# Depthwise convolution of block 2 taken off GpSimd, two channel tiles moved ahead of the attention loop, gates spread anew

## Chip, cores and metric

The kernel runs on 1 core of a Trainium2 chip. The metric is the device time of one launch in microseconds (us). The engines are called by the names of the profile: PE (TensorE), DVE (VectorE), ACT (ScalarE), POOL (GpSimd) and SP (SyncE, whose queue starts most transfers).

## What is computed

Two transformer blocks run one after the other on 512 tokens of width 1024. The change lies in the first half of the second one (`second_block`, one layer). Cut to what matters:

```python
h = modulate(rms_norm_2(x, norm1_g), sh1, sc1)
u = h @ w_in                       # queries, keys/values, conv branch, gates
qn, qr = mla_queries(u[..., :256], q_norm_g, w_uq)          # rms_norm of 256 columns, then w_uq
kn, kr, v = mla_keys(u[..., 256:416], kv_norm_g, w_ukv)     # rms_norm of 128 columns, then w_ukv
attn = attend_blocked(qn, qr, kn, kr, v)                    # 16 heads, 512 queries, 768 keys

a, g = split(u[..., 416:2464])                              # conformer_conv, 1024 channels
y = a * sigmoid(g)
y = depthwise_conv(y, conv_w, 31 taps, centred) + conv_b
y_c = silu(layer_norm(y, ln_g, ln_b)) @ w_pw

g = sigmoid(u[..., 2464:])                                  # 2 x 1024 gates
x = x + g1 * ((g[:1024] * (attn @ w_o_mla) + g[1024:] * y_c) @ w_out)
```

After it comes a product-key expert layer, which the change does not touch.

## The kernel before

Activations lie transposed: 128 channels of a tile on the partitions, the 512 tokens along the free axis. Every float32 matrix product is made from three passes: operand and weight are split into a high part (a copy rounded to fp32r, made by ACT in `split`, L120) and a low part (the difference, made by DVE or POOL in `sub`, L115 or L113), and `lin` runs 8 x 3 = 24 matmuls of 512 columns for one 128-channel output tile. Below, such a group of 24 is called a projection. `load_w` brings a weight tile of 128x1024 through SP and splits it.

`block2` has a prologue, a loop and a tail.

- **Prologue.** The norm of the input is applied (`norm_out`); the key/value latent is projected, its inverse root is made (`rstd`, with ACT's square root and one Newton step on DVE, `newton` L184 to L189) and broadcast over the partitions by small matmuls (`row`, L216). Then come the rotary key, two query tiles `cq` (L886) with a second inverse root, and their splits.
- **Loop.** 16 heads with two units each (`unit`, 256 queries). A unit runs scores on PE, the row maximum on DVE (`mx`, L999), the exponential and the division by the sum on ACT (`pr`), transposes on PE, splits of the transposed weights (`pt`), the product with the values, and one addition into `rc` (L1027), the last DVE instruction of a unit. `prep` makes query, key and value operands of the next head between two units.
- **Filler of the loop.** Twice in a unit, `fill` runs one entry of the list `taps`, and once in a unit one entry of the list `jobs`. The jobs of a channel tile of the convolution are `conv_g` (projection, sigmoid into `y`), `conv_a` (projection, product into `y`) and one or two of the 16 gate projections (`gate`). `conv_a` puts 8 entries on `taps`, each with 2 of the first 16 taps on DVE (L924, L926, summed in place in `z`, the tile `Y` of the profile) and 2 of the other 15 on POOL (a product with a broadcast weight, L929, and an addition, L931). The last entry adds the two halves and adds the tile to `zsum`, on POOL (L933 to L937). Gates in the loop have their low weight part made by POOL (L113).
- **Tail.** Gates that are left run, 3 of them before the layer norm of the convolution and 3 after it; then three stages of eight projections: `w2_omla`, `w2_pw` and `w2_out`.

The order in which the instructions stand on each engine is set when the program is built: a scheduler reorders instructions of the program text within what dependencies and buffers allow. Each engine then runs its own list strictly in that order. The constants that the change touches say how many taps stay on DVE, how many channel tiles get a second gate, and how many gates stay behind the layer norm:

```python
NCV = 16
NGA = 2
NGB = 3
```

Of the kernel before, what the change touches and what calls it, by code (L numbers as in the profile page):

```python
# [8 lines left out]
F32 = mybir.dt.float32  # L9
# [9 lines left out]
P = 128  # L19
# [53 lines left out]
class Kern:  # L73
# [743 lines left out]
    def block2(self, res, r1, r2):  # L817
# [81 lines left out]

        taps = []  # L900

        def conv_g(ct):
            w = self.load_w(a["w2_conv"][8 + ct])
            pg = self.pt("F")
            self.lin([(pg, lat)], w, hh, hl)
            y = self.t(bi, [P, SEQ + 30], F32, "y", bufs=2)
            nc.gpsimd.memset(y[:, :15], 0.0)
            nc.gpsimd.memset(y[:, 15 + SEQ:], 0.0)
            nc.scalar.activation(y[:, 15:15 + SEQ], pg, AF.Sigmoid)
            ys[ct] = y  # L910

        def conv_a(ct):
            w = self.load_w(a["w2_conv"][ct])
            pa = self.pt("F")
            self.lin([(pa, lat)], w, hh, hl)
            y = ys[ct]
            nc.vector.tensor_tensor(y[:, 15:15 + SEQ], pa, y[:, 15:15 + SEQ], op=ALU.mult)  # L917
            zc = z[:, ct]
            zp = self.t(bi, [P, 2, SEQ], F32, "zp")

            def tap(i):
                for j in range(2 * i, min(2 * i + 2, NCV)):
                    if j == 0:
                        nc.vector.tensor_scalar(zc, y[:, :SEQ], cw[:, ct, 0:1], cb[:, ct:ct + 1], op0=ALU.mult, op1=ALU.add)  # L924
                    else:
                        nc.vector.scalar_tensor_tensor(zc, y[:, j:j + SEQ], cw[:, ct, j:j + 1], zc, op0=ALU.mult, op1=ALU.add)  # L926
# [11 lines left out]
            for i in range(8):  # L938
                taps.append(lambda i=i: tap(i))
# [725 lines left out]
```

## Time and profile before

| what | us |
|---|---|
| median of 3 runs (lowest, highest) | 2815.07 (2813.57, 2820.57) |
| the profiled execution: its own time | 2819.39 |
| the profiled execution: span of its trace | 2817.6 |
| PE busy in the span | 2590.9 (92%) |
| DVE busy in the span | 2097.3 (74%) |
| ACT busy in the span | 1196.2 (42%) |
| POOL busy in the span | 1018.9 (36%) |

The rows below come from that one execution. Stretches are given in us from the start of its span. A duration in a row of the timeline reaches a little into the next instruction's start, so the time that an instruction takes from its engine is read from one start to the next.

### The profile page before, as it was taken

The page shows a single profiled execution, that of the slowest core. Times are in us where ns is not written, and L with a number is a line of the kernel's source. Part 1 is how long each engine was busy: PE and PEld are TensorE (multiplying, and loading weights), DVE is VectorE, ACT ScalarE, POOL GpSimd, SP SyncE. Part 2 cuts the span into 40 slices and gives each one's busy share as a digit, 9 for nine tenths or more (in the row PEclk, how much of TensorE's full clock was granted, in tenths as well). Part 3 has the DMA queues.
Part 4 walks back from the last instruction along what each step waited for, and adds up shares of the span by engine and source line. Part 5 has one row for each costly group of instructions (what it writes and reads, how often), then busy time and mean ns, then how long its engine had stood idle before and what let it go on. Part 6 is the DMA issues. An engine that isn't in the chain of part 4 may idle for free. (4 is left out here: it accounts for less than half of the span.)

```text
span 2817.6 us, 38436 instructions
## 1 busy us (share of the span) xinstructions
PE 2590.9 (92%) x14307; PEld 2246.0 (80%) x14307; DVE 2097.3 (74%) x3521; ACT 1196.2 (42%) x1839; POOL 1018.9 (36%) x714
## 2 busy tenths in 40 slices
PE   7899999999988888889998998788899999999998
PEld 6788888887866677777877887777788888888887
DVE  7646677774358898996558777999687888877875
ACT  4445442333245566666342222566433333333332
POOL 0001101110008888882005455554243444444430
PEclk9999999999999999999999999999999999999999
DMA  3210257663331111114433333678999999999993
GB/s 123 70 52 16 91 166 216 215 211 123 114 97 55 51 47 46 50 42 139 144 119 119 116 122 110 227 272 268 326 347 339 340 342 337 339 324 339 332 320 135
DMA packets 218660, 509.99 MB, mean 181 GB/s; under 512 B 23916, under 2 KB 97048, under 8 KB 218344
## 3 DMA queue, kind: packets, MB, share of 16 engines
q1 hardware_dynamic: 168344, 352.23, 37.9%
q0 software_dynamic: 37568, 136.42, 13.8%
q10 hardware_dynamic: 12560, 18.88, 1.8%
q8 instruction: 112, 1.84, 0.3%
q14 instruction: 76, 0.62, 0.1%
HBM read 457.12 MB, written 50.33 MB: 180 GB/s over the span
## 5 line engine op out<-in xcount | busy, mean ns | idle before, releaser
L120 ACT ACTIVATE whi<-wraw 128x1024 fp32r<-128x1024 f32 (+2 forms) x315 | 324.2, 1029 | 597.0 <-PE psU L156 143.5
L115 DVE TENSOR_TENSOR wlo<-wraw,whi 128x1024 fp32r<-128x1024 f32 (+2 forms) x227 | 282.7, 1245 | 155.5 <-ACT whi L120 146.3
L158 PE MATMUL psU<-X,wlo 128*128 128x384 f32 (+1 forms) x1032 | 356.5, 346 | 17.2 <-DVE wlo L115 12.8
L154 PE MATMUL psU<-X,whi 128*128 128x384 f32 (+1 forms) x1032 | 355.5, 345 | 10.3 <-ACT whi L120 8.9
L156 PE MATMUL psU<-Z,whi 128*128 128x384 f32 (+1 forms) x1032 | 354.4, 343 | 0.0
L113 POOL TENSOR_TENSOR wlo<-wraw,whi 128x1024 fp32r<-128x1024 f32 x88 | 222.1, 2526 | 147.3 <-ACT whi L120 143.0
L1169 POOL DMA_INDIRECT row<-v_rows,rsf x128 | 177.0, 1383 | 244.5 <-DVE Y L1188 211.7
L1169 POOL DMA_INDIRECT row<-u_rows,rsf x128 | 167.7, 1310 | 266.7 <-DVE Y L1181 234.3
L120 ACT ACTIVATE wh<-s 128x384 fp32r<-128x384 f32 x128 | 66.9, 525 | 442.5 <-DVE s L1428 436.9
L1446 PE MATMUL psV<-vl,wh 128*128 128x512 f32 x768 | 236.6, 389 | 0.0
L1446 PE MATMUL psV<-vh,wh 128*128 128x512 f32 x768 | 236.5, 389 | 0.0
L1446 PE MATMUL psV<-vh,wl 128*128 128x512 f32 x768 | 236.4, 389 | 0.0
L158 PEld LDWEIGHTS psU<-X,wlo 128*128 128x128 f32 x1032 | 197.5, 191 | 22.1 <-DVE wlo L115 15.2
L154 PEld LDWEIGHTS psU<-X,whi 128*128 128x128 f32 x1032 | 196.7, 191 | 18.1 <-ACT whi L120 12.3
L156 PEld LDWEIGHTS psU<-Z,whi 128*128 128x128 f32 x1032 | 196.7, 191 | 2.8
L1188 DVE SCALAR_TENSOR_TENSOR Y<-row,ckr,Y 128x1024 f32<-128x1024 f32 x128 | 164.0, 1281 | 31.8 <-DMA row<-v_rows,rsf 30.5
L931 POOL TENSOR_TENSOR zp<-zp 128x512 f32<-128x512 f32 x112 | 176.0, 1572 | 8.6
L929 POOL TENSOR_TENSOR zp<-y,cw 128x512 f32<-128x512 f32 x120 | 155.4, 1298 | 63.5 <-DVE y L917 48.4
L1181 DVE SCALAR_TENSOR_TENSOR Y<-row,Y 128x1024 f32<-128x1024 f32 x128 | 158.1, 1235 | 22.8 <-DMA row<-u_rows,rsf 21.9
L1446 PEld LDWEIGHTS psV<-vl,wh 128*128 128x128 f32 x768 | 144.2, 188 | 29.9
L1446 PEld LDWEIGHTS psV<-vh,wl 128*128 128x128 f32 x768 | 144.2, 188 | 29.9
L115 DVE TENSOR_TENSOR vl<-vraw,vh 128x1024 fp32r<-128x1024 f32 x128 | 156.3, 1221 | 13.8 <-ACT vh L120 13.7
(562 smaller groups left out, 6535.7 us busy)
## 6 DMA issues: line engine op xcount, KB each, us to landing
wraw<-w_u SPq DMA_DIRECT2D x128, 512.0 KB, 4.5
vraw<-w_v SPq DMA_DIRECT2D x128, 512.0 KB, 6.6
wraw<-w_mod SPq DMA_DIRECT2D x64, 512.0 KB, 4.2
g_dram<-gs SPq DMA_DIRECT2D x96, 256.0 KB, 5.3
gg<-g_dram SPq DMA_DIRECT2D x32, 768.0 KB, 9.7
wraw<-w_up SPq DMA_DIRECT2D x44, 512.0 KB, 3.6
s_dram<-s ACTq DMA_DIRECT2D x64, 192.0 KB, 1.9
s<-s_dram SPq DMA_DIRECT2D x64, 192.0 KB, 8.1
```

What stands on the lines that cost most here:

```text
L113: self.nc.gpsimd.tensor_tensor(dst, x, f(hi), op=ALU.subtract)
L115: self.nc.vector.tensor_tensor(dst, x, f(hi), op=ALU.subtract)
L120: nc.scalar.activation(hi, src, AF.Copy)
L154: nc.tensor.matmul(o, wh, xh[:, c], start=first, stop=False)
L156: nc.tensor.matmul(o, wh, xl[:, c], start=False, stop=False)
L158: nc.tensor.matmul(o, wl, xh[:, c], start=False, stop=last)
L929: nc.gpsimd.tensor_tensor(zj, y[:, j:j + SEQ], cw[:, ct, j:j + 1].to_broadcast([P, SEQ]), op=ALU.mult)
L931: nc.gpsimd.tensor_tensor(zp[:, 0], zp[:, 0], zj, op=ALU.add)
L1169: nc.gpsimd.indirect_dma_start(out=r, out_offset=None, in_=a[name], in_offset=bass.IndirectOffsetOnAxis(ap=idx[:, k:k + 1], axis=0))
L1181: self.tc.keep_in_program_order(nc.vector.scalar_tensor_tensor(scr, r, 1.0, xt, op0=ALU.mult, op1=ALU.mult, accum_out=sc[:, k:k + 1]))
L1188: self.tc.keep_in_program_order(nc.vector.scalar_tensor_tensor(vacc, r, sc[:, k:k + 1], vacc, op0=ALU.mult, op1=ALU.add))
L1446: nc.tensor.matmul(psv[b][:, h], w[:, c], v[:, h * 512:h * 512 + 512], start=first and w is wh and v is vh, stop=last and w is wl)
```

## The change

All 31 taps of a channel tile run on DVE, four to an entry of `taps` instead of two, and the last entry adds the tile to `zsum` on DVE. POOL keeps only two small memsets per tile. `conv_g` and `conv_a` move up in the text, and tiles 0 and 1 run in the prologue, with ten of their sixteen entries of `taps` run there (`run_taps`); the other six go on in the loop. The list of jobs starts at tile 2, has five places per tile of which one is empty, and takes two gates per tile but the last; so 11 of the 16 gates are in the loop and 5 (`NGB`) stand after the layer norm in the text. All gates have their low weight part made by DVE. The two inverse roots of the prologue are made wholly on DVE (`rstd(..., act=False)` calls `rsqrt`: an integer first guess and four Newton steps, 14 instructions of 4 or 6 columns in place of ACT's root, a reciprocal and three). The squares of `cq` go to the buffer `ql` instead of `y`.

```diff
-NCV = 16
-NGA = 2
-NGB = 3
+NGB = 5
...
+        taps = []
+
+        def conv_g(ct, tag="F"):
+            w = self.load_w(a["w2_conv"][8 + ct])
...
+        def conv_a(ct, tag="F"):
...
+            def tap(i):
+                for j in range(4 * i, min(4 * i + 4, 31)):
+                    if j == 0:
+                        nc.vector.tensor_scalar(zc, y[:, :SEQ], cw[:, ct, 0:1], cb[:, ct:ct + 1], op0=ALU.mult, op1=ALU.add)
+                    else:
+                        nc.vector.scalar_tensor_tensor(zc, y[:, j:j + SEQ], cw[:, ct, j:j + 1], zc, op0=ALU.mult, op1=ALU.add)
+                if i == 7:
+                    if ct == 0:
+                        nc.vector.tensor_copy(zsum, zc)
+                    else:
+                        nc.vector.tensor_tensor(zsum, zsum, zc, op=ALU.add)
...
+        def run_taps(n):
+            for _ in range(n):
+                if taps:
+                    taps.pop(0)()
...
         self.ss_mm(ss, sq, True, True)
+        conv_g(0, "C")
         rs = self.t(bi, [P, KC], F32, "pr", bufs=3)
-        self.rstd(rs, ss, 1.0 / P, bi)
+        self.rstd(rs, ss, 1.0 / P, bi, act=False)
...
                 self.split(kr[r], kb[i][r, 2 * x_], kb[i][r, 2 * x_ + 1])
+        conv_a(0, "C")
+        run_taps(3)
...
             nc.vector.tensor_copy(cq[:, e], pt)
-            self.ss_add(bi, ss, cq[:, e], e, 2, tag="y", wd=SEQ + 30)
+            self.ss_add(bi, ss, cq[:, e], e, 2, tag="ql", wd=SEQ)
+            run_taps(2)
+        conv_g(1, "C")
         rs = self.t(bi, [P, SEQ], F32, "rs")
-        self.rstd(rs, ss, 1.0 / 256, bi)
+        self.rstd(rs, ss, 1.0 / 256, bi, act=False)
...
+        conv_a(1, "C")
+        run_taps(3)
...
-                for j in range(2 * i, min(2 * i + 2, NCV)):
...
-                for j in range(NCV + 2 * i, min(NCV + 2 * i + 2, 31)):
-                    zj = zp[:, 0] if j == NCV else zp[:, 1]
-                    nc.gpsimd.tensor_tensor(zj, y[:, j:j + SEQ], cw[:, ct, j:j + 1].to_broadcast([P, SEQ]), op=ALU.mult)
-                    if j > NCV:
-                        nc.gpsimd.tensor_tensor(zp[:, 0], zp[:, 0], zj, op=ALU.add)
-                if i == 7:
-                    nc.gpsimd.tensor_tensor(zc, zc, zp[:, 0], op=ALU.add)
...
-        def gate(e, lo="pool", tag="F"):
-            w = self.load_w(a["w2_gate"][e], lo_eng=lo)
+        def gate(e, tag="F"):
+            w = self.load_w(a["w2_gate"][e])
...
-        for ct in range(8):
+        for ct in range(2, 8):
             jobs += [lambda ct=ct: conv_g(ct), lambda ct=ct: conv_a(ct)]
-            jobs += [lambda: gate(gates.pop(0)), (lambda: gate(gates.pop(0))) if ct < NGA else (lambda: None)]
+            jobs += [lambda: gate(gates.pop(0)), (lambda: gate(gates.pop(0))) if ct < 7 else (lambda: None), lambda: None]
```

Where the instructions stand, in three places. The first is DVE's list in the prologue, at the inverse root of `cq` (`nwv`, `nwu`, `nwy` are its columns; `Y` is `z`, `y_7435` the input of convolution tile 0). Before:

```order
L209 TENSOR_SCALAR nwv_7557<-psB_7477 128x4
L115 TENSOR_TENSOR wkl_8098<-wkr_8095,wkh_8097 128x128
L115 TENSOR_TENSOR kb_1260_7303<-psA_7611,kb_1260_7303 64x768
L185 RECIPROCAL nwy_7558<-nwy_7558 128x4
L187 TENSOR_TENSOR nwu_7562<-nwv_7557,nwy_7558 128x4
L188 SCALAR_TENSOR_TENSOR nwu_7562<-nwu_7562,nwy_7558 128x4
L189 SCALAR_TENSOR_TENSOR nwy_7558<-nwu_7562,nwy_7558 128x4
L115 TENSOR_TENSOR kb_1260_7303<-psA_7611,kb_1260_7303 64x768
L893 SCALAR_TENSOR_TENSOR cq_7476<-cq_7476,qg_7283,rs_7556 128x512 x2
```

Now:

```order
L207 TENSOR_SCALAR nwv_7697<-psB_7566 128x4
L872 SCALAR_TENSOR_TENSOR Y_7338<-y_7435,cw_1257_7299,Y_7338 128x512
L225 TENSOR_SCALAR nwu_7700<-nwv_7697 128x4
L872 SCALAR_TENSOR_TENSOR Y_7338<-y_7435,cw_1257_7299,Y_7338 128x512
L226 TENSOR_SCALAR nwy_7698<-nwu_7700 128x4
L872 SCALAR_TENSOR_TENSOR Y_7338<-y_7435,cw_1257_7299,Y_7338 128x512
L228 TENSOR_TENSOR nwu_7700<-nwv_7697,nwy_7698 128x4
L872 SCALAR_TENSOR_TENSOR Y_7338<-y_7435,cw_1257_7299,Y_7338 128x512
L229 SCALAR_TENSOR_TENSOR nwu_7700<-nwu_7700,nwy_7698 128x4
L113 TENSOR_TENSOR wlo_7827<-wraw_7825,whi_7826 128x1024
```

Each of the 14 small instructions of the root now has a tap or another long instruction ahead of it: from `nwv` to the last `nwy` stand 18 taps (L872), the first tap of tile 1 (L870), one weight split, two splits of keys and one product into `y`; behind the last `nwy` stand six more taps before the row that normalizes `cq`.

The second place is PE's list at the point where that root is used: `psB` is the broadcast root, `psC` with `cqh` the first head's queries, `psF` a projection, `psC` with `ckv` the first head's values. Before:

```order
L154 MATMUL psF_7639<-X_7301,whi_7634 128x512
L156 MATMUL psF_7639<-Z_7302,whi_7634 128x512
L154 MATMUL psC_7592<-cqh_7571,wqh_7588 128x512
L158 MATMUL psF_7639<-X_7301,wlo_7635 128x512
L156 MATMUL psC_7592<-cql_7572,wqh_7588 128x512
```

Now:

```order
L156 MATMUL psF_7831<-X_7301,wlo_7827 128x512
L214 MATMUL psB_7566<-ident_88,nwy_7698 128x128 x4
L152 MATMUL psC_7784<-cqh_7720,wqh_7780 128x512
L154 MATMUL psC_7784<-cql_7721,wqh_7780 128x512
L156 MATMUL psC_7784<-cqh_7720,wql_7781 128x512
```

Before, ten matmuls of a projection (`psF_7639`), of which the last two are shown, stood between the broadcast and the first query matmul; now nothing does. Ahead of these rows, from the first key/value projection on, PE's list has the projections of tile 0 and tile 1 of the convolution that were not there, and the first one of tile 2 in the place of the first one of tile 0.

The third place is DVE's list in the loop, around the maxima of one unit. Before:

```order
L999 TENSOR_REDUCE mx_9784<-psA_9777 128x1
L1003 RECIPROCAL smx_9705<-smx_9705 128x1
L926 SCALAR_TENSOR_TENSOR Y_7338<-y_9595,cw_1257_7299,Y_7338 128x512
L115 TENSOR_TENSOR wlo_10068<-wraw_10066,whi_10067 128x1024
L1003 RECIPROCAL smx_9787<-smx_9787 128x1
L999 TENSOR_REDUCE mx_9815<-psA_9808 128x1
L926 SCALAR_TENSOR_TENSOR Y_7338<-y_9595,cw_1257_7299,Y_7338 128x512
```

Now:

```order
L1004 TENSOR_REDUCE mx_8305<-psA_8298 128x1
L872 SCALAR_TENSOR_TENSOR Y_7338<-y_7856,cw_1257_7299,Y_7338 128x512
L113 TENSOR_TENSOR wlo_8442<-wraw_8440,whi_8441 128x1024
L1008 RECIPROCAL smx_8308<-smx_8308 128x1
L872 SCALAR_TENSOR_TENSOR Y_7338<-y_7856,cw_1257_7299,Y_7338 128x512
L113 TENSOR_TENSOR wql_8492<-wqr_8489,wqh_8491 128x256
L872 SCALAR_TENSOR_TENSOR Y_7338<-y_7856,cw_1257_7299,Y_7338 128x512
```

Between the first `mx` of the loop and its last `rc`, DVE's list had 120 taps of L926, 7 of L924 and 17 weight splits; now it has 197 taps of L872, 6 of L870, 23 weight splits, 2 splits of tail operands, 7 additions to `zsum` and 4 subtractions of the layer norm's mean. PE's list had some 25.3 projections there and has 22; after the last product with the values it had 4.7 gates ahead of `w2_omla` and has 4. POOL's list in block 2 is 16 memsets.

## Rows read from the trace of the kernel before

**Rows 1.** The page: busy time, share and instructions of each engine.

```profile
PE 2590.9 (92%) x14307; PEld 2246.0 (80%) x14307; DVE 2097.3 (74%) x3521; ACT 1196.2 (42%) x1839; POOL 1018.9 (36%) x714
```

**Rows 2.** Busy by stretch: us, PE, PEld, DVE, ACT, POOL, PEclk, DMA, GB/s.

```profile
797.00:844.00 47.00, 42.49 (x209) 35.03 (x209) 25.41 (x40) 21.29 (x30) 3.74 (x7) 0.96 0.22 72
844.00:1283.00 439.00, 371.54 (x2065) 311.04 (x2064) 386.53 (x519) 270.81 (x474) 372.68 (x268) 0.97 0.16 49
1283.00:1318.00 35.00, 32.65 (x155) 26.41 (x154) 20.83 (x30) 20.46 (x28) 0.25 (x1) 1.00 0.48 149
1318.00:1456.00 138.00, 134.41 (x584) 107.77 (x583) 75.52 (x97) 56.91 (x75) 0.00 (x0) 1.00 0.46 142
```

**Rows 3.** Waits, 843 to 1283: total us, times, longest.

```profile
ACT pr L1002 <- DVE mx L999: 55.8, 28, 5.8
...
PE psB L1012 <- DVE pt L115: 27.9, 16, 3.4
```

**Rows 4.** Timeline of DVE: start, us, instruction; ends of two units.

```profile
1065.16 0.42 DVE L1027 TENSOR_TENSOR rc<-psC,rc 64x256 f32<-64x256 f32 x1 [0.27 <-ACT rc L1026]
...
1118.95 0.42 DVE L1027 TENSOR_TENSOR rc<-psC,rc 64x256 f32<-64x256 f32 x1 [0.24 <-ACT rc L1026]
```

**Rows 5.** Groups of DVE, 840 to 1275: count, busy us, mean ns, idle.

```profile
L926 DVE SCALAR_TENSOR_TENSOR Y<-y,cw,Y 128x512 f32<-128x512 f32 x120 | 147.4, 1229 | 0.7
L115 DVE TENSOR_TENSOR pt<-psB,pt 128x384 fp32r<-128x384 f32 x124 | 64.6, 548 | 10.5 <-ACT pt L120 9.9
...
L115 DVE TENSOR_TENSOR wlo<-wraw,whi 128x1024 fp32r<-128x1024 f32 x16 | 35.9, 2243 | 0.0
...
L115 DVE TENSOR_TENSOR wql<-wqr,wqh 128x256 fp32r<-128x256 f32 x14 | 14.1, 1008 | 0.0
...
L924 DVE TENSOR_SCALAR Y<-y,cw,cb 128x512 f32<-128x512 f32 x8 | 10.9, 1367 | 0.3
```

**Rows 6.** Groups of POOL, 840 to 1275.

```profile
L931 POOL TENSOR_TENSOR zp<-zp 128x512 f32<-128x512 f32 x110 | 172.5, 1568 | 8.5
L929 POOL TENSOR_TENSOR zp<-y,cw 128x512 f32<-128x512 f32 x119 | 154.3, 1300 | 63.4 <-DVE y L917 48.4 <-issue 7.0
```

**Rows 7.** Timeline of DVE: taps and a query weight's split.

```profile
845.04 0.74 DVE L926 SCALAR_TENSOR_TENSOR Y<-y,cw,Y 128x512 f32<-128x512 f32 x1
845.70 0.95 DVE L999 TENSOR_REDUCE mx<-psA 128x1 f32<-128x768 f32 x1
...
1055.45 2.81 DVE L926 SCALAR_TENSOR_TENSOR Y<-y,cw,Y 128x512 f32<-128x512 f32 x2
...
1069.75 0.41 DVE L115 TENSOR_TENSOR wql<-wqr,wqh 128x256 fp32r<-128x256 f32 x1
```

**Rows 8.** Groups of DVE, 400 to 700 (block 1, convolution of 3 taps).

```profile
L115 DVE TENSOR_TENSOR wlo<-wraw,whi 128x1024 fp32r<-128x1024 f32 x46 | 56.2, 1221 | 25.4 <-ACT whi L120 25.4
L428 DVE SCALAR_TENSOR_TENSOR acc<-asb,cw,acc 128x512 f32<-128x512 f32 x40 | 30.0, 749 | 0.7
...
L426 DVE TENSOR_SCALAR acc<-asb,cw,cb 128x512 f32<-128x512 f32 x20 | 10.8, 542 | 0.0
```

**Rows 9.** Timeline of PE in the prologue.

```profile
801.35 2.93 PE L216 MATMUL psA<-ident,nwy 128*128 128x128 f32 x12 [2.09 <-DVE nwy L189]
...
836.25 0.48 PE L154 MATMUL psF<-X,whi 128*128 128x512 f32 x1
...
841.90 0.51 PE L154 MATMUL psA<-kb,qh 128*128 128x384 f32 x2
```

**Rows 10.** Timeline of DVE in the prologue.

```profile
826.53 0.16 DVE L209 TENSOR_SCALAR nwv<-psB 128x4 f32<-128x4 f32 x1 [0.83 <-PE psB L203]
...
828.28 0.16 DVE L189 SCALAR_TENSOR_TENSOR nwy<-nwu,nwy 128x4 f32<-128x4 f32 x1
...
830.49 1.41 DVE L893 SCALAR_TENSOR_TENSOR cq<-cq,qg,rs 128x512 f32<-128x512 f32 x2 [0.89 <-ACT rs L219]
...
844.17 0.94 DVE L999 TENSOR_REDUCE mx<-psA 128x1 f32<-128x768 f32 x1
```

More of the change, by code (lines that the diff above doesn't have):

```diff
@@ L848, in proj @@
             return pt[:, 0]
+        taps = []
+        def conv_g(ct, tag="F"):
+            w = self.load_w(a["w2_conv"][8 + ct])
+            pg = self.pt(tag)
+            self.lin([(pg, lat)], w, hh, hl)
+            y = self.t(bi, [P, SEQ + 30], F32, "y", bufs=2)
+            nc.gpsimd.memset(y[:, :15], 0.0)
+            nc.gpsimd.memset(y[:, 15 + SEQ:], 0.0)
+            nc.scalar.activation(y[:, 15:15 + SEQ], pg, AF.Sigmoid)
+            ys[ct] = y
+        def conv_a(ct, tag="F"):
+            w = self.load_w(a["w2_conv"][ct])
+            pa = self.pt(tag)
+            self.lin([(pa, lat)], w, hh, hl)
+            y = ys[ct]
+            nc.vector.tensor_tensor(y[:, 15:15 + SEQ], pa, y[:, 15:15 + SEQ], op=ALU.mult)
+            zc = z[:, ct]
+            def tap(i):
[9 more added lines that the diff above has]
+                        nc.vector.tensor_tensor(zsum, zsum, zc, op=ALU.add)
+            for i in range(8):
+                taps.append(lambda i=i: tap(i))
+        def run_taps(n):
+            for _ in range(n):
+                if taps:
+                    taps.pop(0)()
+        ys = {}
+        zsum = self.t(self.cp, [P, NF], F32, "rsg")[:, :SEQ]
         pl, pt = self.pt("A")[:, 0], self.pt("F")
@@ L898, in block2 @@
             nc.sync.dma_start(cse[x_], a["c_cs"][:, x_])
[L900 to L921, printed above, removed]
-                for j in range(2 * i, min(2 * i + 2, NCV)):
[L923 to L926, printed above, removed]
-                for j in range(NCV + 2 * i, min(NCV + 2 * i + 2, 31)):
-                    zj = zp[:, 0] if j == NCV else zp[:, 1]
-                    nc.gpsimd.tensor_tensor(zj, y[:, j:j + SEQ], cw[:, ct, j:j + 1].to_broadcast([P, SEQ]), op=ALU.mult)
-                    if j > NCV:
-                        nc.gpsimd.tensor_tensor(zp[:, 0], zp[:, 0], zj, op=ALU.add)
-                if i == 7:
-                    nc.gpsimd.tensor_tensor(zc, zc, zp[:, 0], op=ALU.add)
-                    if ct == 0:
-                        nc.gpsimd.tensor_copy(zsum, zc)
-                    else:
-                        nc.gpsimd.tensor_tensor(zsum, zsum, zc, op=ALU.add)
-            for i in range(8):
-                taps.append(lambda i=i: tap(i))
         def small_w(src, n, tag):
@@ L1036, in gate @@
             nc.scalar.dma_start(self.sg_dram[:, e], sg)
-        ys = {}
-        zsum = self.t(self.cp, [P, NF], F32, "rsg")[:, :SEQ]
         jobs = []
-        for ct in range(8):
+        for ct in range(2, 8):
             jobs += [lambda ct=ct: conv_g(ct), lambda ct=ct: conv_a(ct)]
-            jobs += [lambda: gate(gates.pop(0)), (lambda: gate(gates.pop(0))) if ct < NGA else (lambda: None)]
+            jobs += [lambda: gate(gates.pop(0)), (lambda: gate(gates.pop(0))) if ct < 7 else (lambda: None), lambda: None]
         gates = list(range(16))
@@ L1060, in block2 @@
         while len(gates) > NGB:
-            gate(gates.pop(0), "dve", "CF"[len(gates) % 2])
+            gate(gates.pop(0), "CF"[len(gates) % 2])
         ln = self.t(bi, [P, 2, SEQ], F32, "cq")
@@ L1073, in block2 @@
         while gates:
-            gate(gates.pop(0), "dve", "CF"[len(gates) % 2])
+            gate(gates.pop(0), "CF"[len(gates) % 2])
         def packed():
```

## Prediction

> **What bounds the kernel now.** First the page's busy times [rows 1]: PE works 92% of the span, so it is the engine to save time on, but an average over stages says nothing of one stage. So next the busy time by stretch [rows 2]. In the tail of block 2 (1318 to 1456) PE works 134.4 of 138 us: PE is the bound there. In the attention loop (844 to 1283, 439 us) it is not: PE works 371.5 us, DVE 386.5, POOL 372.7, ACT 270.8. No engine is full, two are close to it, and DVE is the fullest. Who waits there [rows 3]: ACT waits 55.8 us for row maxima and PE 27.9 us for splits, both made by DVE. The ends of two units [rows 4] are four units apart and 53.8 us, 13.5 us a unit; one channel tile of the convolution takes such a period. So the loop is paced by DVE's list, with PE close behind, and what an instruction costs on DVE is what counts.
>
> The groups of DVE and of POOL in the loop [rows 5, 6] show something odd. A tap takes 1229 ns on average, a weight split 2243, a split of query weights 1008, but the splits from PSUM take 548 for 384 columns. The timeline [rows 7] has one tap of 0.74 us and, with POOL at work, two of 2.81 us together, so 1.4 each; one query split takes 0.41. Block 1 runs the same forms with POOL nearly idle [rows 8]: 749 ns a tap, 1221 a weight split, 542 the first tap. So DVE instructions whose operands all lie in SBUF take about twice as long while POOL's tensor instructions run, and those that read PSUM don't. POOL's 326.8 us of taps [rows 6] are paid for by DVE a second time.
>
> **The change part by part.** DVE prices are from start to start, which is 0.07 us below the duration: 0.74 began at 845.04 and its successor at 845.70 [rows 7].
>
> *DVE in the loop*, from first `mx` to last `rc`, counts from the order. Taps: 120 x (1.229 - 0.07) = 139 before; 197 x 0.67 = 132 now: -7. First taps: 7 x 1.30 = 9; 6 x 0.47 = 3: -6. Weight splits: 16 x 2.17 = 35 in the row's window; 25 (two are tail operands) x 1.15 = 29: -6. Query splits: 14 x 0.94 = 13; 14 x 0.34 = 5: -8. New are 7 additions to `zsum` and 4 subtractions, 11 x 0.67: +7. Together -20: 386.5 becomes about 366, although DVE takes over all of POOL's taps of six tiles. Two more kinds of SBUF splits (`ql`, `wkl`) also shrink; I leave them out. The ends for an unseen price: if a tap stays at 1.229, the loop's DVE grows by 77 x 1.16 = 89 instead; if all fall to block 1's prices, it is the sum above. The rows of block 1 are of the same form, so I take them.
>
> *PE in the loop*: 24 matmuls take 5.65 us (836.25 to 841.90 [rows 9]). 25.3 - 22 = 3.3 projections leave: -18.6, to 353.
>
> *The loop's length.* With today's idle times kept, DVE would need 366 + 52.5 = 418 and PE 353 + 67.5 = 420. But PE's 67.5 us of idle hold 27.9 us of waiting for DVE splits [rows 3], and what stands ahead of a split is mostly a tap or a weight split of twice its proper length. If such waits halve, some 14 us of PE's idle go: 406. I take 405, so 34 below 439. Ends: 383, where DVE is busy 366 of 383 us, and 420. The last four units have neither taps nor jobs left to hide waits; that is why I stay away from the low end.
>
> *The prologue* pays for it. Four projections move ahead of the first maximum: 4 x 5.65 = +22.6 on PE. The first fills PE's wait of 2.09 us for the first inverse root and 0.9 us after it [rows 9]: -3. The second root gets slow: from `nwv` to the last Newton step took 826.53 to 828.44 [rows 10], 1.9 us. Now 18 taps x 0.67 = 12.1, a weight split 1.15, a first tap 0.47, three PSUM instructions of 0.6 to 0.9 and 13 small ones of 0.1 to 0.2 stand in that stretch: 17 to 18 us. PE has meanwhile 15 matmuls of a projection, two whole ones and the first keys, 3.5 + 11.3 + 1 = 16, so it waits 1 to 3 us. Then six taps (4.0) stand ahead of the normalization, which with the split takes 2.7, and PE's next instruction is the query matmul that needs them: 5 to 6 us more with nothing to run. Sum +22.6 - 3 + 8 = +27: the first maximum goes from 844.2 [rows 10] to about 871. Ends +20 (PE's waits covered) and +34 (they double). The 20 extra small instructions of the two roots are in these waits; ACT's two roots of 4 and 6 columns were never late. SP loads the moved weights earlier in its list; four more of 512 KB fit where the stretch 797 to 844 uses 0.22 of the DMA engines [rows 2].
>
> *The tail.* PE has 4 gates instead of 4.7 ahead of `w2_omla`: -4. The sum of the convolution is complete some units before the loop ends, so the layer norm starts earlier and PE's 2.4 us of idle between 1283 and 1318 [rows 2] mostly go: -2. Together -6 (ends -2 and -9). Behind that PE is full already and keeps its list.
>
> *POOL* loses its taps and ten gate splits; nobody in the loop waited much for it, so that alone is worth nothing.
>
> Sum: +27 - 34 - 6 = -13 on the profiled execution of 2819.4 us, 2806; the median of the runs lies 4.3 below that execution, so the forecast is **2802 us**.
>
> **A rule that speaks against it.** The rows show a busy DVE whose neighbour made it slower [rows 5, 7, 8]. The Trainium skill (Perfetto Trace Analysis, section Optimizing Scalar/DVE Operations) says that when VectorE is saturated, moving work to GpSimd may make sense, and adds that the two share an SBUF read port, so that it might not help. By its first half alone this change, which moves work the other way, would be the last rival below; the trace agrees with its second half, at 1229 against 749 ns for a tap [rows 5, 8].
>
> **The rivals.** About what a measurement of this kernel can tell from no change is 0.3%, 8.4 us.
>
> - *The pace stays, only the work leaves* (chance 0.25). PE and DVE wait for each other as before, whatever the single instruction takes: loop 420, prologue +30. +30 - 19 - 6 = +5: 2820, no measurable change. For it: ACT and PE form a chain through every unit that taps don't shorten. Against: waits of up to 5.8 us for one maximum [rows 3] are too long for anything but a queue.
> - *The waits go almost wholly* (0.13). DVE runs at its best share seen in 50 us of the loop, about 0.94, throughout: loop 366/0.94 = 389, with a prologue of +22: 22 - 50 - 6 = -34: 2781.
> - *The prologue eats it all* (0.10). DVE's list is strictly in order, and 43 taps stand in it ahead of the first `mx`. If PE's waits behind the second root and the sigmoid of tile 2, which needs a buffer of tile 0's taps, double, the first maximum comes at 878; with a loop of 420 the sum is +34 - 19 - 4 = +11: 2826, slower. It decides from a first maximum later than 875 with a loop of over 420.
> - *The taps don't get faster* (0.03). If 1.2 us is what a tap in place costs beside PE and ACT, the loop grows by 89 and the prologue by 43 x 0.5: over 2900. Against it stand single taps of 0.74 in the loop itself [rows 7].
>
> **How the numbers follow.** The forecast has 0.49. Faster by over 0.3% (below 2806.6): the forecast and the second rival, 0.62. Within 0.3%: 0.25. Slower: the two last rivals, 0.13. The range takes the forecast with its ends, goes down to the second rival and up to the third: 2779 to 2826; some 0.2 lie outside.
>
> **What would show it.** Right: no POOL tensor instruction between 780 and 1456; a median tap of about 0.73 us and weight splits of 1.22; first `mx` near 871, last `rc` near 1276; PE without idle from there to 1456 minus 13. DVE's share in the loop about 0.9. Wrong: taps over 1 us; a first maximum after 880; units that still take 13.5 us with DVE below 0.85, which would say that PE and ACT pace them; or a stretch of PE idle behind `psB` of over 10 us.

## The result, and the profile after

The changed kernel takes 2792.7 us, median of four runs (2790.1 to 2797.2), beside 2817.8 (2813.6 to 2823.6) for the kernel before on the same chip: ratio 0.990 (95% interval 0.988 to 0.992), 25 us faster, where 2802 was forecast from a median of 2815.1: 13 less. The profiled executions differ by 22.2 us of span (2817.6 and 2795.4); 20.4 of them lie in these places. The loop is counted from the start of the first row maximum to that of the last `rc`, the tail from there to the last addition into `x2`.

| | first maximum | loop | last `rc` | tail | `x2` done |
|---|---|---|---|---|---|
| before | 844.2 | 438.4 | 1282.6 | 169.2 | 1451.8 |
| after | 876.1 | 386.3 | 1262.4 | 169.0 | 1431.4 |
| difference | +31.9 | -52.1 | -20.1 | -0.2 | -20.4 |
| forecast | +27 | -34 | -7 | -6 | -13 |

Busy times by stretch of the kernel after (us, PE, PEld, DVE, ACT, POOL, PEclk, DMA, GB/s) answer to [rows 2]:

```profile
797.00:876.00 79.00, 69.08 (x305) 55.52 (x304) 63.40 (x112) 26.58 (x35) 0.16 (x2) 0.89 0.20 70
876.00:1262.00 386.00, 355.69 (x1992) 301.85 (x1990) 356.49 (x611) 264.16 (x469) 0.79 (x10) 0.96 0.17 54
1262.00:1297.00 35.00, 31.86 (x127) 25.59 (x128) 16.24 (x25) 19.03 (x27) 0.00 (x0) 0.83 0.32 107
1297.00:1431.00 134.00, 134.00 (x581) 108.11 (x579) 71.94 (x90) 52.24 (x67) 0.00 (x0) 1.00 0.43 144
```

In the loop POOL went from 372.7 us to nothing, DVE's list from 386.5 to 356.5, PE's from 371.5 to 355.7. DVE works 92% of the loop instead of 88, PE 92 instead of 85. The groups of DVE from 876 to 1262 (count, busy us, mean ns, idle ahead) answer to [rows 5]:

```profile
L872 DVE SCALAR_TENSOR_TENSOR Y<-y,cw,Y 128x512 f32<-128x512 f32 x198 | 145.6, 741 | 0.8
L113 DVE TENSOR_TENSOR pt<-psB,pt 128x384 fp32r<-128x384 f32 x128 | 66.4, 550 | 7.8 <-ACT pt L118 6.5
...
L113 DVE TENSOR_TENSOR wlo<-wraw,whi 128x1024 fp32r<-128x1024 f32 x23 | 28.0, 1216 | 0.2 <-ACT whi L118 0.2
...
L113 DVE TENSOR_TENSOR wql<-wqr,wqh 128x256 fp32r<-128x256 f32 x14 | 5.8, 411 | 0.0
```

A tap costs 741 ns instead of 1229, a weight split 1216 instead of 2243, a query split 411 instead of 1008; the split from PSUM stays at 550. DVE does 78 more taps than before in less time (145.6 us beside 147.4). The waits of the loop, as in [rows 3]:

```profile
ACT pr L1007 <- DVE mx L1004: 30.0, 24, 2.7
...
PE psB L1017 <- DVE pt L113: 1.3, 2, 0.8
```

PE's wait behind `psB` for DVE's splits fell from 27.9 to 1.3 us and ACT's for maxima from 55.8 to 30.0. The prologue's second root, on DVE's timeline, answers to [rows 10]:

```profile
835.43 0.16 DVE L207 TENSOR_SCALAR nwv<-psB 128x4 f32<-128x4 f32 x1
835.52 0.75 DVE L872 SCALAR_TENSOR_TENSOR Y<-y,cw,Y 128x512 f32<-128x512 f32 x1
836.19 0.16 DVE L225 TENSOR_SCALAR nwu<-nwv 128x4 int32<-128x4 int32 x1
...
854.35 0.15 DVE L230 SCALAR_TENSOR_TENSOR nwy<-nwu,nwy 128x4 f32<-128x4 f32 x1
```

From `nwv` to the last step it is 19 us where it was 1.9, a tap or something longer behind nearly every small step. On PE's timeline one sees what waits for it, and one thing more:

```profile
854.55 2.07 PE L214 MATMUL psB<-ident,nwy 128*128 128x128 f32 x8 [3.18 <-DVE nwy L230]
859.85 0.79 PE L152 MATMUL psC<-cqh,wqh 128*128 128x512 f32 x1 [3.23 <-ACT cqh L118]
...
862.14 0.63 PE L152 MATMUL psC<-cqh,wqh 128*128 128x512 f32 x1
```

Behind the two waits a matmul of 512 columns takes 0.63 us instead of 0.40; the granted clock of the stretch is 0.89 (0.96 in [rows 2]).

### The profile page after: what moved, and what is told of

It is laid out like the page before. It is cut to its first block, busy times and chain, and to the rows that moved or that the text cites. A ratio compares the mean times of both kernels' runs of the same rounds, so it can differ in the third digit from the quotient of the medians.

```text
span 2795.4 us, 38357 instructions
## 1 busy us (share of the span) xinstructions
PE 2605.2 (93%) x14307; PEld 2261.8 (81%) x14307; DVE 2095.3 (75%) x3679; ACT 1191.2 (43%) x1833; POOL 647.2 (23%) x456
## 5 line engine op out<-in xcount | busy, mean ns | idle before, releaser
L111 POOL TENSOR_TENSOR wlo<-wraw,whi 128x1024 fp32r<-128x1024 f32 x78 | 199.6, 2561 | 137.8 <-ACT whi L118 133.6
L872 DVE SCALAR_TENSOR_TENSOR Y<-y,cw,Y 128x512 f32<-128x512 f32 x240 | 176.1, 741 | 1.0
L1449 PEld LDWEIGHTS psV<-vh,wh 128*128 128x128 f32 x768 | 143.5, 188 | 25.2
```

What stands on the lines that cost most here:

```text
L111: self.nc.gpsimd.tensor_tensor(dst, x, f(hi), op=ALU.subtract)
L1449: nc.tensor.matmul(psv[b][:, h], w[:, c], v[:, h * 512:h * 512 + 512], start=first and w is wh and v is vh, stop=last and w is wl)
```

## The experiments

Theories: **A**, the loop lasts as long as its fuller list over some 0.92, so what matters is how much DVE and PE have to do there (a list's share is its busy time over the length of the loop); **B**, POOL's presence makes PE and ACT wait, whatever the length of the lists. The prologue is counted from the first root's `nwv` to the first maximum, since what lies ahead of it differs by up to 7 us between these executions (e3_pool_load apart, where POOL works there already); the last three columns are busy us in the loop's stretch. All stretches come from the one profiled execution of each kernel, the ratios from all its runs.

| kernel | ratio to before (interval) | prologue | loop | tail | sum | PE | DVE | POOL |
|---|---|---|---|---|---|---|---|---|
| before | 1 | 44.9 | 438.4 | 169.2 | 652.5 | 371.5 | 386.5 | 372.7 |
| after | 0.990 (0.988, 0.992) | 75.6 | 386.3 | 169.0 | 631.0 | 355.7 | 356.5 | 0.8 |
| e1_vec_only | 0.990 (0.989, 0.992) | 46.0 | 408.5 | 173.9 | 628.3 | 373.2 | 384.5 | 1.0 |
| e2_move_only | 1.013 (1.011, 1.015) | 77.6 | 439.8 | 168.8 | 686.3 | 364.8 | 374.0 | 326.6 |
| e3_pool_load | 1.019 (1.016, 1.021) | 147.1 | 380.8 | 168.4 | 696.3 | 348.2 | 356.4 | 0.8 |
| e9_pool_in_loop | 1.008 (1.007, 1.010) | 76.1 | 434.8 | 168.9 | 679.8 | 370.7 | 403.4 | 158.6 |
| e8_half_taps | 0.978 (0.976, 0.980) | 75.6 | 349.2 | 168.8 | 593.6 | 338.1 | 299.7 | 0.8 |
| e10_gate_low_on_pool | 0.989 (0.987, 0.991) | 44.0 | 411.8 | 170.1 | 625.9 | 374.4 | 384.4 | 24.0 |
| e4_roots_act | 0.989 (0.987, 0.991) | 72.9 | 380.7 | 168.6 | 622.3 | 346.9 | 355.9 | 0.8 |
| e5_after_again | 0.989 (0.987, 0.991) | 76.1 | 383.5 | 169.0 | 628.6 | 352.1 | 356.9 | 0.8 |
| e7_taps_later | 0.987 (0.985, 0.989) | 65.3 | 384.8 | 168.5 | 618.6 | 350.4 | 361.1 | 0.8 |
| e6_jobs_to_end | 0.988 (0.986, 0.990) | 72.4 | 384.0 | 168.3 | 624.7 | 350.0 | 350.0 | 0.8 |
| e11_taps_into_tail | 0.991 (0.989, 0.993) | 72.1 | 350.0 | 202.6 | 624.7 | 333.7 | 331.3 | 0.6 |
| e12_gates_first | 0.984 (0.982, 0.986) | 73.6 | 351.5 | 188.4 | 613.5 | 334.8 | 331.0 | 0.6 |

**One half of the change alone.** The kernel before, with its taps and gates' low parts on DVE:

```diff
-                for j in range(2 * i, min(2 * i + 2, NCV)):
+                for j in range(4 * i, min(4 * i + 4, 31)):
...
-        def gate(e, lo="pool", tag="F"):
+        def gate(e, lo="dve", tag="F"):
```

> The kernel before with all 31 taps of all eight tiles, and the gates' low parts, on DVE; no tile is moved, both roots stay on ACT. Theory A (the loop lasts as long as the fuller of DVE's and PE's lists over about 0.92, as it does after the change: 356.5 of 386 us): DVE's list is the 356.5 us of the changed kernel plus two tiles at 24 us (30 taps of 0.67, four operands of 1.15, about 2 for the rest), 404; loop 404/0.92 = 439, so as long as before, and the sum is 2810 to 2822 us: no change. Taps have a median near 0.74 us all the same. Theory B (what cost was the waiting that POOL's presence made, not the length of the list): the loop loses most of the 52 us that the change gained there, 390 to 405, and the time is near 2780 us, since nothing was added ahead of it.

The time fell as far as with the whole change. The loop of e1_vec_only by stretch, its taps, and PE's longest wait in it with its only one behind DVE's `pt`:

```profile
847.00:1255.00 408.00, 373.24 (x2078) 314.36 (x2077) 384.49 (x652) 270.22 (x474) 0.95 (x12) 0.97 0.17 52
```

```profile
L924 DVE SCALAR_TENSOR_TENSOR Y<-y,cw,Y 128x512 f32<-128x512 f32 x239 | 177.3, 743 | 1.2
```

```profile
PE psA L154 <- ACT pr L994: 22.4, 17, 4.5
...
PE psC L1013 <- DVE pt L115: 0.8, 4, 0.2
```

Theory A's 404 us for DVE was miscounted: most of the second moved tile's taps run in the changed kernel's loop, so the moved tiles are worth 28 us there, not 48. With the measured 384.5 us the loop is DVE's list at a share of 0.94. But the kernel before has nearly the same two lists (386.5 and 371.5 us) and 30 us more of loop: B holds for that comparison, though its own 390 to 405 us of loop and its 2780 us were missed as well. PE's wait behind `psB` for `pt`, 27.9 us before, has no row left; the longest is for the scores that ACT's exponential still reads. POOL's 372.7 us of work had saved DVE nothing: with them DVE's list was 2 us longer.

**The other half alone**: the tiles moved and the gates respread, convolution and gates' low parts shared with POOL as before.

```diff
+                for j in range(NCV + 2 * i, min(NCV + 2 * i + 2, 31)):
+                    nc.gpsimd.tensor_tensor(zj, y[:, j:j + SEQ], cw[:, ct, j:j + 1].to_broadcast([P, SEQ]), op=ALU.mult)
```

> The changed kernel's places (two tiles ahead of the loop, gates spread anew) with the convolution split between DVE and POOL as before, the gates' low parts on POOL in the loop, and the roots on ACT. Theory A (length of the lists): DVE in the loop has the 386.5 us of before less two tiles at 24 us at the doubled prices (15 taps of 1.16, a first tap of 1.30, two PSUM reads, two operands of 2.17), 339; PE has 355 and is the fuller one: loop about 355/0.92 = 386, as after the change; first maximum 870 to 878; time 2788 to 2800 us. Theory B (POOL's presence makes the waits): PE's waits for DVE's splits and ACT's for maxima stay, the loop keeps PE's 67 us of idle, 415 to 422, and with 25 to 30 us more ahead of it the time is 2815 to 2826 us.

1.3% slower than before, 2858.4 us, beyond both ranges. A fell: DVE and PE had less to do in the loop than before and it took as long. DVE's group of taps, then PE's waits for POOL, a kind the kernel before does not have:

```profile
L875 DVE SCALAR_TENSOR_TENSOR Y<-y,cw,Y 128x512 f32<-128x512 f32 x100 | 136.9, 1370 | 1.0
```

```profile
PE psF L157 <- POOL wlo L112: 11.0, 3, 5.3
```

The two halves don't add. By the sums of the table, moving costs 34 us while POOL works, and nothing that one execution each can tell once it is quiet (631.0 and 628.6 against 628.3). Why this loop is even longer than B's 415 to 422 stays open; the 11 us behind POOL's queue are part of it.

**POOL's price by itself.** POOL multiplies into a scratch tile, beside an unchanged rest.

```diff
+                if ct > 1:
+                    for u in range(2):
+                        nc.gpsimd.tensor_tensor(zp[:, u], cse[0], cse[1], op=ALU.mult)
```

> The changed kernel, and beside each group of four taps of the loop's six tiles two multiplications of 128x512 on POOL from constants into a scratch tile that nobody reads: 96 instructions, about 125 us of POOL in the loop at the 1.3 us of before. If a tensor instruction of POOL slows DVE's SBUF-only ones by sharing something with them, whatever they compute: taps of 0.74 us that stand alone and taps of 1.2 to 1.4 beside one of these, mean tap in the loop 0.88 to 0.95; DVE's busy time in the loop rises by 30 to 45 us from 356 and the loop by as much, to 415 to 430; the PSUM splits of 384 columns stay at 0.55. If the slow taps of before were due to DVE and POOL working on the same tiles of y: mean tap 0.74, loop 386, no change.

Ratio 1.019 (1.016 to 1.021), but not by the loop: nothing held the multiplications there, and they ran in one piece from 792.5 to 945 us; the first maximum came at 960, and the loop behind it, with POOL quiet, is about as long as without them (380.8 us). So neither forecast can be read off, but the prologue shows the price undisturbed. DVE's timeline in it, POOL's beside it, then POOL's group:

```profile
813.34 2.33 DVE L113 TENSOR_TENSOR wlo<-wraw,whi 128x1024 fp32r<-128x1024 f32 x1
...
816.89 1.22 DVE L228 TENSOR_TENSOR nwu<-nwv,nwy 128x6 f32<-128x6 f32 x1
818.14 0.17 DVE L229 SCALAR_TENSOR_TENSOR nwu<-nwu,nwy 128x6 f32<-128x6 f32 x1
818.34 1.13 DVE L230 SCALAR_TENSOR_TENSOR nwy<-nwu,nwy 128x6 f32<-128x6 f32 x1
```

```profile
814.55 2.28 POOL L878 TENSOR_TENSOR zp<-cs,cs 128x512 f32<-128x512 f32 x1
...
816.79 1.29 POOL L878 TENSOR_TENSOR zp<-cs,cs 128x512 f32<-128x512 f32 x1
```

```profile
L878 POOL TENSOR_TENSOR zp<-cs,cs 128x512 f32<-128x512 f32 x96 | 152.1, 1620 | 6.7 <-DMA cs<-c_cs 6.3
```

An instruction on six columns takes 1.13 to 1.22 us, and in the same chain 0.17 when it slips through: it waits for whole POOL instructions. The one of 816.89 ends at 818.11, as the POOL instruction of 816.79 does (818.08). Then the same load tied to the loop, by an operand that the tile's own taps read:

```diff
-                        nc.gpsimd.tensor_tensor(zp[:, u], cse[0], cse[1], op=ALU.mult)
+                        nc.gpsimd.tensor_tensor(zp[:, u], y[:, :SEQ], cse[0], op=ALU.mult)
```

> As e3_pool_load, but the 96 multiplications on POOL read the tile's own gated values, so that they come where the tile's taps come, inside the loop. In the kernel before, 268 POOL instructions raised DVE's busy time in the loop by about 100 us over the prices it has alone, 0.37 us each. So here DVE's 356 us become 385 to 400. DVE's list alone (e8_half_taps: 57 us of list less, 35 us of loop less, 0.6 us each) gives a loop of 384 + 22 = 400 to 412. If longer single instructions also make PE and ACT wait longer at equal lists (the kernel before against e1_vec_only: 386.5 and 384.5 us of DVE, 438 and 408 us of loop, 30 us for 268 instructions), the loop is 410 to 425, PE's waits behind psB grow, and the time is 2817 to 2830 us; by the list alone 2806 to 2817. First maximum 874 to 877 in both.

Its groups of DVE, its longest wait of PE, and its loop by stretch:

```profile
L875 DVE SCALAR_TENSOR_TENSOR Y<-y,cw,Y 128x512 f32<-128x512 f32 x198 | 176.0, 894 | 0.8
L113 DVE TENSOR_TENSOR pt<-psB,pt 128x384 fp32r<-128x384 f32 x128 | 66.3, 548 | 6.1 <-ACT pt L118 5.2
...
L1014 DVE RECIPROCAL smx<-smx 128x1 f32<-128x1 f32 x64 | 9.5, 153 | 1.2 <-ACT pr L1013 1.0
...
L873 DVE TENSOR_SCALAR Y<-y,cw,cb 128x512 f32<-128x512 f32 x6 | 8.3, 1390 | 0.0
```

```profile
PE psB L1023 <- DVE pt L113: 17.7, 8, 6.1
```

```profile
876.00:1311.00 435.00, 370.65 (x1993) 310.31 (x1991) 403.39 (x611) 265.25 (x470) 158.59 (x106) 0.93 0.15 48
```

96 useless POOL instructions gave DVE 47 us more (0.49 each, not 0.37) and the loop 48 to 51, beyond both forecasts; PE's wait behind `psB` came back from 1.3 to 17.7, and PE's own work grew by 15 us on as many matmuls, at a granted clock of 0.93. That the loop grew by what DVE's list grew by fits A (the share is 0.93 again); the price was put too low. It is no matter of shared tiles: in e3_pool_load POOL read only constants and wrote what nobody reads.

**Which list bounds the quiet loop.** Every second tap of the loop's six tiles left out.

```diff
-                for j in range(4 * i, min(4 * i + 4, 31)):
+                for j in range(4 * i, min(4 * i + 4, 31), 1 if ct < 2 else 2):
```

> The changed kernel with every second tap of the loop's six tiles left out (16 of 31 are done; the result is another): 90 taps of 0.67 us, 60 us, leave DVE's list of 356 us in the loop; PE's list stays at 355. Theory G (since POOL is quiet, PE's own list sets the loop, with the share of 0.92 to 0.945 that it has in both kernels without POOL): loop 376 to 386 instead of 386. Theory H (DVE's list still sets it): the loop falls until PE is full, 358 to 368.

Below both ranges, on H's side: DVE's 57 us less took 34 to 37 off the loop, until PE was full:

```profile
873.00:1223.00 350.00, 338.06 (x1993) 291.70 (x1991) 299.72 (x522) 264.18 (x471) 0.79 (x10) 1.00 0.20 60
```

PE's own list shrank with it, from the changed kernel's 352 to 356 us to 338, on as many matmuls: the granted clock is 1.00 instead of 0.96 to 0.97. The floor is 350, not the 358 that H took from rows at a lower clock. So the quiet loop is about as long as DVE's list over 0.91 to 0.95, or PE's over 0.95 to 0.97, whichever is more (all rows of the table with POOL under 25 us). The ranges are no finer than that: e6_jobs_to_end, below, has 6 us less on DVE than e4_roots_act and a loop 3 us longer.

**A small offload** from e1_vec_only back to POOL, the gates' low parts alone.

```diff
-        def gate(e, lo="dve", tag="F"):
+        def gate(e, lo="pool", tag="F"):
```

> As e1_vec_only (all taps on DVE, no tile moved), but the low parts of the loop's ten gates stay on POOL as before the change. DVE's list is shorter by 10 operands of 1.15 us, 11.5, and each POOL operand of about 2.4 us delays two or three SBUF instructions beside it, 0.6 to 1.2 us in all. If a small offload pays: DVE 380 to 382 instead of 384.5 in spite of that, loop 3 to 7 us shorter than 408.5, time 2788 to 2793 us. If what POOL takes off is given back as in the convolution: DVE 383 to 387, loop 406 to 412, ratio to the kernel before 0.989 to 0.992 as e1_vec_only.

Given back to the last microsecond: DVE 384.4 instead of 384.5, its taps 787 ns instead of 743. Its taps and POOL's group in the loop:

```profile
L924 DVE SCALAR_TENSOR_TENSOR Y<-y,cw,Y 128x512 f32<-128x512 f32 x239 | 187.6, 787 | 1.2
```

```profile
L113 POOL TENSOR_TENSOR wlo<-wraw,whi 128x1024 fp32r<-128x1024 f32 x9 | 23.1, 2568 | 245.8 <-ACT whi L120 114.7 <-DVE smx L995 38.6 <-DVE kb L115 34.6
```

**The prologue's price.** First the roots.

```diff
-        self.rstd(rs, ss, 1.0 / 256, bi, act=False)
+        self.rstd(rs, ss, 1.0 / 256, bi)
```

> The changed kernel with both inverse roots of the prologue as before (square root on ACT, reciprocal and one Newton step on DVE: 5 DVE instructions instead of 15 each). In the changed kernel the second root took 19 us because one tap stands behind each of its small steps. Theory C (the root's steps hold PE up): the second root takes 8 to 10 us, PE's 3.2 us of idle ahead of the broadcast and part of the 3.2 behind it go, the first maximum comes 4 to 9 us earlier, 867 to 872, and the time is 2784 to 2789 us. Theory D (it is the amount of taps and projections ahead of the first maximum): the taps that stood in the root stand behind it, the first maximum stays within 2 us of 876, and ACT's changes of its table (about 1.3 us each) cost what is gained: 2791 to 2796 us.

The second root took 7.3 us, less than C's 8 to 10, and the first maximum came at 872.4, half a microsecond past C's range; the median of 2790.7 lies between the two ranges and can't be told from the changed kernel's. On top of that, the taps are handed out behind the root:

```diff
-            run_taps(2)
...
-        run_taps(3)
+        run_taps(10)
```

> The changed kernel with both roots on ACT (as e4_roots_act), and the ten groups of taps of the prologue handed out behind the second root instead of before and within it. Theory C (the steps of the root stand behind taps, and PE waits for them): the second root takes 5 to 6 us, the first maximum comes at 866 to 870 us instead of 872.5, the loop stays at 381 to 384, and 2 to 6 us are gained on e4_roots_act. Theory D (the taps have to be done somewhere): the first maximum comes as early, but the loop is longer by as much, 384 to 388, and the time that of e4_roots_act within 2 us.

The second root took 4.8 us. The prologue is 7.6 us shorter than in e4_roots_act and the loop 4.1 longer. But that is not what C meant: PE from the first `nwv` to the first maximum, in e4_roots_act and here,

```profile
799.51:872.45 72.94, 63.92 (x286) 51.98 (x286) 59.47 (x91) 26.71 (x35) 0.16 (x2) 0.93 0.22 75
...
804.59:869.92 65.33, 57.51 (x264) 47.45 (x264) 53.81 (x81) 26.99 (x35) 0.16 (x2) 0.95 0.19 65
```

has 22 matmuls fewer, nearly a projection, which run in the loop now (2012 there instead of 1990). Its work fell by 6.4 us, its idle time by 1.2. So what PE waited for the root's steps is about a microsecond of the 7.6, and D describes the rest, with a projection beside the taps. For scale, the changed kernel once more, on the same chip:

> The changed kernel once more, on one chip with the next three, so that they can be set against it. Its ratio to the kernel before was 0.990; the same is expected, 0.988 to 0.992, with the first maximum at 876 and the last unit's end at 1262 us of the profile.

It repeated (0.989), its loop 383.5 instead of 386.3, so 3 us of a loop are chance. Both edits together make the sum of the block 10 us shorter in the profiles (628.6 and 618.6); the medians, 2791.4 and 2789.0, lie too close to confirm it.

**The tail.** With e4_roots_act's roots, the eleven gates are spread so that the last units keep projections.

```diff
-            jobs += [lambda: gate(gates.pop(0)), (lambda: gate(gates.pop(0))) if ct < 7 else (lambda: None), lambda: None]
+            jobs += [lambda: gate(gates.pop(0)), lambda: None]
+        jobs += [lambda: gate(gates.pop(0)), lambda: None] * 5
```

> The changed kernel with both roots on ACT (as e4_roots_act), and the same eleven gates and twelve convolution projections spread so that the last five units of the loop still have three projections between them; in the changed kernel the last four units have none. Theory E (units without a projection to fill them let PE wait, and the clock granted to it falls to half behind that, which is where the tail's gain of 6 us went): granted clock 1.00 from 1240 us to the loop's end and 0.95 or more in the 35 us behind it; 3 to 7 us less than e4_roots_act between the first maximum and the last addition of the block; time 2783 to 2788 us. Theory F (PE has the same list, and a unit that gives up a projection now waits elsewhere): within 2 us of e4_roots_act, 2788 to 2793 us.

The granted clock in the 35 us behind the loop was 0.90 instead of 0.85, the tail 0.3 us shorter than in e4_roots_act, the loop no shorter. The time is F's; but E's condition, a clock of 0.95 or more there, did not come about, so E is not excluded.

**Towards a better version.** If DVE binds the loop and PE the tail, taps belong in the tail. The kernel is e4_roots_act with a third buffer for the gated tile and `NTL = 46` groups of taps handed out in the loop's 64 fills:

```diff
+                fills[0] += 1
+                nt = fills[0] * NTL // 64 - (fills[0] - 1) * NTL // 64
```

> The changed kernel with both roots on ACT (as e4_roots_act), a third buffer for the gated tile, and 46 instead of 54 groups of taps handed out in the loop: the last 30 or so taps are done behind the last unit, where DVE works 72 of 134 us and PE is full with gates and w2_omla that need no convolution. DVE's list in the loop is 20 to 24 us shorter (24 taps by the order, and six more that spread less densely). If DVE's list sets the loop at 0.6 us each and the layer norm still ends before w2_pw needs it: loop 366 to 374 instead of 381 to 384, tail 168 to 171, time 2776 to 2784 us, ratio 0.983 to 0.986. If the layer norm comes too late for PE: tail 175 to 185 and no gain, 2786 to 2792 us.

The loop fell further than forecast, to 350, where PE's share is 0.95, and the tail ate it: 202.6 us. The median of 2800.4 lies beyond both ranges; the profiled execution of the table is 9 us below it. PE behind the last unit:

```profile
1256.53 2.07 PE L1074 MATMUL psB<-rsg,ones 128*128 128x512 f32 x2 [16.72 <-DVE rsg L878]
...
1267.87 0.80 PE L153 MATMUL psC<-X,whi 128*128 128x512 f32 x1 [7.99 <-ACT nt L1041]
```

Gates that need no convolution stood in PE's queue behind the sum that does. So, on top of that, the gates go ahead of it:

```diff
-NGB = 5
+NGB = 0
```

> As e11_taps_into_tail, with all five remaining gates ahead of the convolution's layer norm instead of two. There the loop took 350 us and the stretch behind it 202.6 instead of 169, since PE's next instruction after two gates was the sum of the convolution, for whose taps it waited 16.7 us, and 8.0 behind it, with three gates queued behind. Five gates take 28 us, as long as the taps do. If that queue was the whole loss: loop 350 to 354, the stretch behind it 170 to 182, profile span 2762 to 2775 us and ratio to the kernel before 0.977 to 0.983, the fastest of all here. If the loss comes back in another place (DVE has taps, gates' operands, layer norm and w2_omla's operands in one list there, and PE waits for the operands): the stretch behind the loop 185 to 200, span 2776 to 2788 us, ratio 0.984 to 0.990.

The fastest median of all that compute the whole, 2780.9 us (2775.8 to 2782.7), 0.984 of the time before. But the tail is the second forecast's, 20 us longer than in e4_roots_act. The tails of e4_roots_act and of this kernel:

```profile
1253.19:1421.80 168.61, 165.64 (x706) 133.37 (x706) 88.20 (x115) 70.95 (x93) 0.00 (x0) 0.97 0.43 137
...
1228.26:1416.60 188.34, 173.22 (x734) 138.74 (x734) 113.86 (x148) 75.24 (x99) 0.00 (x0) 0.95 0.43 136
```

8 of the 20 are PE's own work: 28 matmuls more, a projection that left the loop with the taps (so 5 to 6 us of the loop's gain, an estimate from 5.65 us a projection, were only moved), and a lower clock. 11 are one wait on PE, behind a product on DVE that waited for ACT:

```profile
1301.46 0.80 PE L153 MATMUL psC<-kb,whi 128*128 128x512 f32 x1 [11.31 <-DVE Y L1120]
```

```profile
1300.71 0.69 DVE L1120 TENSOR_TENSOR Y<-psC,pr 128x512 f32<-128x512 f32 x1 [4.07 <-ACT pr L1115]
```

```profile
1298.76 1.28 ACT L1115 ACT_TABLE_LOAD   x1 [2.92 <-DMA pr<-sg_dram]
```

The gates' values are loaded into the three `pr` buffers through which the convolution's Silu runs, and that now ends late: the first load starts at 1295.28, while the last of these buffers are still being split. It also stands in SP's list behind a weight load of 1294.63; which of the two held it is not shown, and other buffers were not tried.

## Why the prediction was right, and where it was not

**Right** was what carried it: POOL's tensor instructions make DVE's SBUF-only ones slower, taps fall to about 0.73 us and weight splits to 1.22, and the loop gains more than the prologue loses. e9_pool_in_loop shows the cause without any other edit; the last rival (taps stay slow) is out.

**The loop's term was too small: -34 forecast, -52 measured.** e1_vec_only takes it apart. With lists as long as before, the loop lost 30 us (438.4 to 408.5); the shorter lists took 22 more (to 386.3). The list's part was sized well: 439 to 418 or 420 with the idle times kept. The mis-sized step is "if such waits halve, some 14 us of PE's idle go": PE's wait behind `psB` went from 27.9 to 1.3 us, PE's whole idle time in the loop from 67.5 to 30.3. ACT's waits for maxima did about halve. DVE's list fell by 30, not 20: `ql` and `wkl`, left out, gave 5.8 us by the groups of both kernels, two products into `y` that moved with their tiles 1.4, and the loop before has 17 weight splits (37.1 us), where the 16 of the row's window were counted. The loop's length is that of the second rival (389), but not quite for its reason: it is 356.5 us of DVE at a share of 0.92, not 366 at 0.94, two misses that cancel.

**The step "that alone is worth nothing" was wrong as a reading of the change.** No row of the loop before has PE waiting for POOL, but POOL's silence is all of the gain: e1_vec_only has it without a moved tile. Moving two tiles takes 22 us off the loop (408.5 to 386.3) and 5 off the tail, and puts 30 on the prologue. The prediction booked the moved work as a gain of the loop (DVE 366 and PE 353 us) without setting the sum of a kernel that moves nothing beside it.

**The prologue's term: +27 forecast, +31.9 measured**, 1.2 of it ahead of the first root. From 797 on, PE's busy time rose by 26.6: the four projections of 22.6, and 4.0 for matmuls at the lower clock, which the sum did not have. PE's idle time rose by 5.4 (4.5 to 9.9), where -3 + 8 had been put: the sum came out, its parts did not. The waits at the second root were 3.2 and 3.2 instead of 1 to 3 and 5 to 6, with smaller ones behind them. The first root's waits (2.09 and 0.90) gave back 1.5 and not 3, since ACT loaded a table and did the new sigmoid ahead of the root's copy, and PE waited 1.5 us for that. First maximum at 876 is past the third rival's 875; its other condition, a loop over 420, did not hold.

**The tail's term: -6 forecast, -0.2 measured.** The fewer matmuls came: 706 in the tail instead of 728, and still 166.05 us of PE's work instead of 166.06, since the granted clock fell, a term that the sum did not have. It fell in the 35 us behind the loop: 127 matmuls took 31.9 us at a granted clock of 0.83, where 155 took 32.7 at 1.00. PE's 2.4 us of idle time there did not go either (3.1). The two tails:

```profile
1282.56:1451.80 169.24, 166.06 (x728) 133.06 (x726) 93.96 (x121) 74.47 (x99) 0.69 (x1) 1.00 0.46 145
...
1262.42:1431.40 168.98, 166.05 (x706) 133.60 (x706) 88.18 (x114) 71.05 (x93) 0.00 (x0) 0.97 0.41 136
```

Ahead of the tail, in the last units, PE had not been busy, and the clock was at the lower of its two levels (0.50: 1.2 of 2.4 GHz). Slices of 6 us of the kernel after show it:

```profile
1246.00:1252.00 6.00, 3.92 (x20) 2.78 (x20) 4.81 (x10) 5.88 (x12) 0.00 (x0) 0.81 0.14 36
1252.00:1258.00 6.00, 5.42 (x20) 3.90 (x18) 3.67 (x6) 3.48 (x6) 0.00 (x0) 0.50 0.26 80
1258.00:1264.00 6.00, 4.61 (x18) 3.88 (x18) 4.05 (x7) 3.74 (x7) 0.00 (x0) 0.50 0.28 89
```

Filling those units was tried in e6_jobs_to_end, which raised the clock behind the loop only to 0.90 and took 0.3 us off the tail; what a full clock there would give back was not measured.

**The sum was nearer than its terms, by luck.** The loop gave 18 us more than forecast, and the prologue and the tail together took 11 more; so the block came out 7 us from its forecast.

**Open**: with POOL fully at work (before, e2_move_only) DVE's share is 0.85 to 0.88, below the 0.93 of e9_pool_in_loop, so 23 us of the one (386.5/0.93 is 415.6 of 438.4) and 38 of the other are neither list's. The share falls as the mean tap grows: 0.91 to 0.95 at 0.74 to 0.79 us (where DVE bounds the loop), 0.93 at 0.89, 0.88 at 1.23, 0.85 at 1.37. That would fit waits behind longer single instructions, but POOL's own queue and the order of DVE's list change with it, and no run separates them.

## What to carry to other kernels

Price an offload by what it adds to the engine that it relieves: here each POOL instruction gave DVE 0.37 (the estimate ahead of e9_pool_in_loop) to 0.49 us back (measured there), and 373 us of POOL's work saved it nothing. Read the share of each list first with the neighbour quiet; the loop then follows the fuller list, and work taken from it gains only as far as the stage that it goes to has room: two tiles with their projections took 22 us off the loop and put 30 on the prologue. And what stands in an in-order queue behind a late result is late too, however independent: the gates cost e11_taps_into_tail 14 us against e12_gates_first.

## What the hardware showed that was not expected

The slowdown is a wait for whole instructions, not shared bandwidth: six columns cost 1.13 to 1.22 us instead of 0.17, while in e9_pool_in_loop a reciprocal of one SBUF operand (153 ns) and the splits from PSUM (548) are untouched. The Trainium skill (SBUF — State Buffer, section Who interferes with whom) says that a DVE instruction with two SBUF inputs contends with a GpSimd instruction that reads SBUF, that one with at most one SBUF input does not outside the two-port modes, and that the pair of ports is a lock held for an instruction. These rows agree, the first tap too: it has one tensor operand, took 1390 ns instead of 537, and is a TENSOR_SCALAR, an operation that the section lists among those that can take the lock.

POOL pays as well: its multiplication of 128x512 took 1.29 us beside an instruction of six columns in e3_pool_load, 2.28 beside a weight split of DVE that began before it (813.34) and ended at 815.67, and 1.62 on average.

And DVE's list bears on PE's clock: with 57 us less of it the same 1993 matmuls of the loop took 338 us instead of 352 to 356, at a granted clock of 1.00 instead of 0.96 to 0.97; with 47 us more (e9_pool_in_loop) they took 371 at 0.93. It is not the list alone: e4_roots_act and e7_taps_later have the changed kernel's list within 5 us, at 0.98 and 0.99.
